# Inverses emitted in slices of four steps, keys' transposes as a stream of their own

## The chip, the cores and the metric

One core of a Trainium2 chip runs the kernel. The metric is the device time of one execution in microseconds (us), the median of three timed runs. One more execution was recorded by the hardware profiler; its trace is what is read here. "us" without a further word is time on the chip. The kernel also has a clock of its own, which exists only while the program is written out; its microseconds are called planned us.

## What is computed

One inference step of a hybrid decoder layer, for a prompt of 1024 tokens and 8 sequences of 4 new tokens, with model width 1024. The part around the change is the RWKV-7 branch with 16 heads of 64:

```python
def step(S, inp):                       # one token, all heads
    r_t, w_t, k_t, a_t, b_t, v_t = inp
    sa = jnp.einsum('bhij,bhj->bhi', S, a_t)
    S = S * w_t[:, :, None, :] + sa[..., :, None] * b_t[..., None, :] + v_t[..., :, None] * k_t[..., None, :]
    y = jnp.einsum('bhij,bhj->bhi', S, r_t)
    return S, y

z = rmsnorm(x) @ w_in                   # convolution, r/k/v/lora and gate columns
ya = conformer_conv(z) @ w_conv_out
yb = gated(group_norm(wkv7_scan(...))) @ w_rw_out
x = x + (sigmoid(g1) * ya + sigmoid(g2) * yb) @ w_mix_out
x = x + conv_ffn(rmsnorm(x))            # 1024 -> 6144 -> 3072 -> 1024
```

## The kernel before

The token recurrence is done in chunks of 64 tokens. In a chunk the recurrence is a triangular system, and its 64x64 matrix is inverted: two 32x32 diagonal blocks are inverted by forward substitution on VectorE, and the off-diagonal block is made from them on TensorE. The stage that does this, `mixer_b`, goes through 16 units (n = 0 to 15); a unit is four heads by 256 tokens, so it has 16 chunk matrices and 32 diagonal blocks of 32x32.

What a unit goes through, with the lines of the profile:

- `prep` (lines 880 to 985): five loads, decays and scaled keys E and BK on VectorE, ScalarE and GpSimd. It holds two waits, 6.0 and 8.0 planned us. Unit n may only start when chain n-3 is done.
- `stage` (from line 992): 16 matmuls of BK and E with 128 columns ("the keys"), evicted and masked into LQ (lines 1005 to 1013). Then the 32 diagonal blocks go to memory (dL, line 1019), come back as one 512 KB load that spreads each block over the partitions four times over (L, line 1021), and the substitution runs in 31 steps of two VectorE instructions, a product tm (line 1028) and a sum into X (line 1030), each step needing the step before. X goes to SBUF through ScalarE (Xs, line 1032), to memory (dX, line 1034) and back into LQ (line 1038). Last, BK is turned by 8 transposes in two halves, each after 0.5 planned us, and v by 4 more after a wait for chain n-2.
- `combine` (from line 1061): VectorE transposes of LQ (D11, line 1068), then two rounds of 16 matmuls with 32 columns.
- `chain` (from line 1090): the four chunks of a unit, one after another, each with four rounds of small matmuls and VectorE evictions between them (R, UV), because the state passes from chunk to chunk and from unit to unit.
- `group_norm`, the samples' own work, the layer norm of the convolution branch.

Each of these is a Python generator, a stream. `drive` writes the program: it asks the first stream in its list whose due time has come to emit its next piece, and when none is due it emits three matmuls of a filler, the weight projections of r, k, v and of the gates (`project_g`). The clock is advanced by each matmul's columns over 2.4 GHz, four times that for plain float32 operands. `yield 500` means: not before 0.5 planned us from now. A stream that waits for another's mark looks every 0.4 planned us (`wait`). Fillers remain to be emitted after the last chain.

The order in which code is emitted isn't the order on an engine. The tile framework hands the program to a scheduler that fills each engine's queue; where two instructions could go, the one emitted first goes first. On the chip each queue is then fixed and runs in order. All loads and stores are issued from SyncE (SP). The buffers that matter: one L, one tm, one Xs, one X in PSUM; three each of E, BK and LQ; two UV; two PSUM banks "w" that nearly every small product shares.

The streams and their list:

```python
self.drive([self.s_chain(), self.s_comb(), self.s_stage(), self.s_norm(), self.s_prep(), self.s_samples(), self.s_ln(), self.s_y(), self.s_shift()],
           self.fillers())
```

Of the kernel before, what the change touches and what calls it, by code (L numbers as in the profile page):

```python
# [31 lines left out]
class Net:  # L32
# [638 lines left out]
    def mixer_b(self):  # L671
        nc, a = self.nc, self.a
        self.wkv_consts()
        self.t2_left = self.T2N
        self.want = 0
        self.t_stage = {}
        self.st, self.pr, self.ch = {}, {}, {}
        with ExitStack() as e:
            self.t4 = self.pool(e, "t4b", 2)
            self.t2 = self.pool(e, "t2", self.T2N)  # L680
            self.e_sg = ExitStack()
            self.sg = self.pool(self.e_sg, "stage", 3, side="right")
            self.ln = self.pool(e, "lanes", 1)
            self.sm = self.pool(e, "small", 2)
            sp = self.pool(e, "samples")
            self.sG, self.sQK = (sp.tile([128, 4, 64], F32, name=x) for x in ("sG", "sQK"))
            self.sbv = sp.tile([128, 4, 32], F32, name="sbv")
            self.sUV = sp.tile([128, 8, 64], F32, name="sUV")
            self.sPC = sp.tile([128, 8, 8], F32, name="sPC")
            dram = lambda nm, m, w: [self.dr.tile([m, w], F32, name=f"{nm}{i}") for i in range(ND)]  # L690
            self.d_BT, self.d_S = dram("d_BT", 64, 128), dram("d_S", 128, 512)
            self.d_bv = [self.dr.tile([128, 2, TP], F32, name=f"d_bv{i}") for i in range(ND // 2)]
            self.drive([self.s_chain(), self.s_comb(), self.s_stage(), self.s_norm(), self.s_prep(), self.s_samples(), self.s_ln(), self.s_y(), self.s_shift()],
                       self.fillers())
            self.e_sg.close()

# [49 lines left out]
    def s_stage(self):  # L746
        for n in range(self.NH):
# [3 lines left out]
            self.done.add(("stage", n))  # L751
            self.t_stage[n] = self.clock

    def s_comb(self):
        for n in range(self.NH):
            yield from self.wait(("stage", n))
            yield max(0, self.t_stage[n] + self.TINV - self.clock)
            yield from self.combine(n)
            self.done.add(("comb", n))
# [227 lines left out]
    W_NIN, W_BV, W_GN, W_STAGE = 6000, 8000, 12000, 0  # L987
    W_LN = 14000
    SQ = (1, 1, 2, 1)
    TINV = 29750  # L990

    def stage(self, n):

        nc = self.nc
        E, BK, PC, nin, v = self.pr[n]
        LQ = self.sg.tile([128, 8, 128], F32, tag="LQ", name="LQ")
        for g in range(2):
            c4 = slice(4 * g, 4 * g + 4)
            for x in range(2):
                p, q = slice(64 * x, 64 * x + 64), slice(64 - 64 * x, 128 - 64 * x)  # L1000
                ps = self.pw_tile()
                pv = ps.rearrange("p (c t) -> p c t", t=128)
                for c in range(4):
                    self.mm(pv[:, c], BK[p, 4 * g + c], E[x][p, 4 * g + c], True, True)
                nc.vector.tensor_tensor(out=LQ[p, c4, 0:64], in0=pv[p, :, 0:64],
                                        in1=nin[p, c4].rearrange("p (c o) -> p c o", o=1).to_broadcast([64, 4, 64]), op=ALU.mult)
                nc.scalar.activation(out=LQ[p, c4, 64:128], in_=pv[p, :, 64:128], func=AF.Copy)  # L1007
                nc.scalar.activation(out=E[x][q, c4], in_=pv[q], func=AF.Copy)
                for w in (LQ[p, c4], E[x][q, c4]):
                    w = w.rearrange("p c (q t) -> p c q t", q=2)  # L1010
                    nc.gpsimd.affine_select(out=w, in_=w, pattern=[[0, 4], [1, 2], [1, 64]], compare_op=ALU.is_ge, fill=0.0,  # L1011
                                            base=-1, channel_multiplier=-1)
                yield 500

        dL = self.dr.tile([2, 2, 8, 32, 32], F32, name=f"dL{n}")
        dX = self.dr.tile([8, 4, 32, 32], F32, name=f"dX{n}")
        for x in range(2):
            for d in range(2):
                nc.sync.dma_start(out=dL[x, d].rearrange("c i j -> i c j"), in_=LQ[64 * x + 32 * d:64 * x + 32 * d + 32, :, 32 * d:32 * d + 32])
        L = self.ln.tile([128, 32, 32], F32, tag="L", name="L")  # L1020
        nc.sync.dma_start(out=L, in_=dL.rearrange("(o h) d c i j -> o (h d c) (i j)", o=1).to_broadcast([4, 32, 1024]))

        X = self.pw.tile([128, 512], F32, tag="x", name="x", bufs=1)[:, 0:256].rearrange("p (a t) -> p a t", t=32)
        tm = self.ln.tile([128, 8, 32], F32, tag="tm", name="tm")
        nc.vector.tensor_copy(out=X, in_=self.x0)
        for s in range(31):
            a, m = s // 4 + 1, 31 - s
            nc.vector.tensor_tensor(out=tm[:, :a, :m], in0=L[:, s:s + 1, s + 1:32].to_broadcast([128, a, m]),  # L1028
                                    in1=X[:, :a, s:s + 1].to_broadcast([128, a, m]), op=ALU.mult)
            nc.vector.tensor_tensor(out=X[:, :a, s + 1:32], in0=X[:, :a, s + 1:32], in1=tm[:, :a, :m], op=ALU.add)  # L1030
        Xs = self.ln.tile([128, 8, 32], F32, tag="X", name="X")
        nc.scalar.activation(out=Xs, in_=X, func=AF.Copy)
        for q in range(4):
            nc.sync.dma_start(out=dX[:, q].rearrange("a l t -> l a t"), in_=Xs[32 * q:32 * q + 32])
        for x in range(2):
            for d in range(2):
                p = 64 * x + 32 * d
                nc.sync.dma_start(out=LQ[p:p + 32, :, 32 * d:32 * d + 32],
                                  in_=dX.rearrange("a q l t -> (a q) l t")[:, 16 * x + 8 * d:16 * x + 8 * d + 8])

        for g in range(2):
            yield 500
            ps = self.pw_tile()
            for c in range(4):
                self.tr(ps[:, c * 128:(c + 1) * 128], BK[:, 4 * g + c], self.ident)
            nc.scalar.activation(out=BK[:, 4 * g:4 * g + 4], in_=ps.rearrange("p (c t) -> p c t", t=128), func=AF.Copy)
        yield from self.wait(*([("chain", n - 2)] if n > 1 else []))
        UV = self.sg.tile([128, 8, 2, 64], F32, tag="UV", name="UV", bufs=2)
        ps = self.pw_tile()
        for m in range(4):  # L1050
            self.tr(ps[:, m * 128:(m + 1) * 128], v[:, m // 2, m % 2 * 128:m % 2 * 128 + 128], self.ident)
        pv = ps.rearrange("p (m x t) -> p m x t", m=4, x=2)
        uv = UV.rearrange("p (m o) x t -> p m o x t", o=2)
        for o in range(2):
            for x in range(2):
                q = slice(64 - 64 * x, 128 - 64 * x)
                nc.scalar.activation(out=uv[q, :, o, x], in_=pv[64 * o:64 * o + 64, :, x], func=AF.Copy)
        self.st[n] = (E, LQ, BK, UV)
        self.t2_left += 1
# [622 lines left out]
```

## Time and profile before

| | |
|---|---|
| median of three runs | 2564.65 us |
| lowest, highest | 2553.85, 2574.9 us |
| the profiled execution's own time | 2538.03 us |
| its span in the trace | 2536.3 us |
| mean granted TensorE clock over the span | 0.926 |
| TensorE busy | 2367.6 us |
| VectorE busy | 1427.9 us |

The span is the time from the first to the last recorded instruction; 1.7 us of the execution lie around it. A granted clock of 1.00 is 2.4 GHz, 0.50 is 1.2 GHz, and a value between is a stretch that had both. PE is TensorE's matmuls, PEld its weight loads, DVE VectorE, ACT ScalarE, POOL GpSimd, SP the engine that issues the transfers. An entry such as "[5.07 <-DMA L<-dL]" says that the engine stood idle for 5.07 us before that instruction and what released it.

### The profile page before, as it was taken

What the parts mean: (1) busy time and instruction counts of PE and PEld (TensorE: products, weight loads), DVE (VectorE), ACT (ScalarE), POOL (GpSimd) and SP (SyncE); (2) the same over time, 40 slices, a digit from 0 to 9 for tenths busy, and PEclk for the clock granted to TensorE, in tenths of its full rate; (3) what the DMA queues carried; (4) which work ended last, traced back from release to release, by engine and by line L of the source; (5) the groups of instructions that cost most, each with busy time, mean ns of one, the idle gap of its engine ahead of it and who ended that gap; (6) DMA issues with size and microseconds to landing.
All of it is one profiled execution on the core that took longest, in us unless ns stands there. A gap on an engine that the chain in (4) does not pass through costs nothing.

```text
span 2536.3 us, 41660 instructions
## 1 busy us (share of the span) xinstructions
PE 2367.6 (93%) x16094; PEld 2140.9 (84%) x16094; DVE 1427.9 (56%) x3588; ACT 918.7 (36%) x1748; POOL 909.1 (36%) x879
## 2 busy tenths in 40 slices
PE   5889989999788799999989999999999999999998
PEld 4878888777676677777777899999999999999998
DVE  5799955586646674555464434465444534445345
ACT  4133433354244354454434322333222222223125
POOL 3332253244324443443333243433323323323333
PEclk9899987898688698999779999999999999999999
DMA  3223443243233333533323854431111111111111
GB/s 104 56 60 130 171 149 89 81 121 93 78 89 79 93 107 83 140 98 94 94 64 96 273 178 131 128 128 44 44 47 48 44 51 44 47 48 41 54 46 75
DMA packets 307640, 230.64 MB, mean 91 GB/s; under 512 B 90492, under 2 KB 287123, under 8 KB 306921
## 3 DMA queue, kind: packets, MB, share of 16 engines
q1 hardware_dynamic: 307185, 227.80, 31.1%
q8 instruction: 127, 2.08, 0.4%
q14 instruction: 72, 0.59, 0.1%
q0 software_dynamic: 256, 0.17, 0.0%
HBM read 157.45 MB, written 70.45 MB: 90 GB/s over the span
## 4 chain that ended last, share of the span: by engine, by line
PE 66%; DVE 7%; DMA 7%; POOL 3%; issue 2%; ACT 1%; SPq 1%; POOLq 0%; DVEq 0%; ACTq 0%
PE mm L54 52%; PE w L54 7%; DMA L<-dL 4%; PE c L54 2%; PE y L54 2%; PE w L61 2%; DVE tm L1028 1%; DVE x L1030 1%; DVE t L961 1%; DMA ga<-d_ga 0%; POOL BK L982 0%; POOL wlo L49 0%; POOL LQ L1011 0%; DVE lnQ L666 0%; DVE v L486 0%
## 5 line engine op out<-in xcount | busy, mean ns | idle before, releaser
L54 PE MATMUL mm<-hH,whi 128*128 128x352 f32 (+1 forms) x2568 | 887.6, 346 | 27.0 <-DVE bcol L496 11.2
L54 PE MATMUL mm<-hL,whi 128*128 128x352 f32 (+1 forms) x2568 | 866.2, 337 | 0.2 <-DVE hL L248 0.2
L54 PE MATMUL mm<-hH,wlo 128*128 128x352 f32 (+1 forms) x2568 | 862.7, 336 | 0.0
L54 PEld LDWEIGHTS mm<-hH,whi 128*128 128x128 f32 (+1 forms) x2568 | 499.4, 194 | 55.9 <-issue 14.1
L54 PEld LDWEIGHTS mm<-hL,whi 128*128 128x128 f32 (+1 forms) x2568 | 500.9, 195 | 11.2 <-DVE hL L248 0.5
L54 PEld LDWEIGHTS mm<-hH,wlo 128*128 128x128 f32 (+1 forms) x2568 | 500.6, 195 | 8.7 <-issue 0.2
L49 POOL TENSOR_TENSOR wlo<-wraw,whi 128x1024 fp32r<-128x1024 f32 (+2 forms) x123 | 292.5, 2378 | 462.0 <-ACT whi L48 427.9
L48 ACT ACTIVATE whi<-wraw 128x1024 fp32r<-128x1024 f32 (+2 forms) x123 | 126.0, 1025 | 366.8 <-PE mm L54 270.1
L1544 DVE SCALAR_TENSOR_TENSOR c<-u,par,c 128x1024 f32<-128x1024 f32 x96 | 167.0, 1739 | 55.6 <-ACT c L1540 55.6
L359 DVE SCALAR_TENSOR_TENSOR sg<-cu,par,sg 128x1024 f32<-128x1024 f32 x120 | 185.1, 1550 | 3.4 <-ACT sg L357 1.7
L1514 DVE TENSOR_TENSOR u<-mm,rs 128x352 f32<-128x352 f32 x144 | 73.2, 509 | 186.5 <-PE mm L54 186.3
L54 PE MATMUL mm<-fH,whi 128*128 128x352 f32 x504 | 163.4, 324 | 0.0
L1569 DVE TENSOR_TENSOR acc<-mm,acc 128x352 f32<-128x352 f32 x168 | 86.8, 523 | 135.0 <-PE mm L54 135.0
L54 PE MATMUL mm<-fH,wlo 128*128 128x352 f32 x504 | 162.7, 323 | 0.0
L54 PE MATMUL mm<-fL,whi 128*128 128x352 f32 x504 | 162.7, 323 | 0.0
L1028 DVE TENSOR_TENSOR tm<-L,x 128x60 f32<-128x60 f32 (+24 forms) x496 | 99.4, 200 | 79.7 <-DMA L<-dL 72.5
L1030 DVE TENSOR_TENSOR x<-x,tm 128x60 f32<-128x60 f32 (+24 forms) x496 | 105.0, 212 | 7.0
L1525 POOL COPY lr<-u 128x2 f32<-128x2 f32 x48 | 9.0, 187 | 276.3 <-DVE u L1514 267.6
L54 PE MATMUL w<-E,BK 64*128 64x128 f32 x512 | 90.7, 337 | 8.8 <-DVE tm L1028 3.4
L1011 POOL TENSOR_SCALAR_AFFINE_SELECT LQ<-LQ 64x512 f32<-64x512 f32 x64 | 44.1, 690 | 148.3 <-ACT LQ L1007 146.8
L54 PEld LDWEIGHTS mm<-fH,whi 128*128 128x128 f32 x504 | 94.8, 188 | 0.5
L54 PEld LDWEIGHTS mm<-fH,wlo 128*128 128x128 f32 x504 | 95.0, 188 | 0.0
(379 smaller groups left out, 3971.2 us busy)
## 6 DMA issues: line engine op xcount, KB each, us to landing
wraw<-w_in SPq DMA_DIRECT2D x50, 512.0 KB
wraw<-w_up SPq DMA_DIRECT2D x48, 512.0 KB
wraw<-w_down SPq DMA_DIRECT2D x32, 384.0 KB
L<-dL SPq DMA_DIRECT2D x16, 512.0 KB
d_alr<-la SPq DMA_DIRECT2D x8, 528.0 KB
d_cum<-lc SPq DMA_DIRECT2D x8, 528.0 KB
d_gout<-lg SPq DMA_DIRECT2D x8, 528.0 KB
d_k<-k SPq DMA_DIRECT2D x8, 528.0 KB
```

The costliest lines, as they stand in the source:

```text
L48: nc.scalar.activation(out=hi[:, :nk, :m], in_=raw[:, :nk, :m], func=AF.Copy)
L49: (lo_eng or nc.gpsimd).tensor_tensor(out=lo[:, :nk, :m], in0=raw[:, :nk, :m], in1=hi[:, :nk, :m].bitcast(F32), op=ALU.subtract)
L54: self.nc.tensor.matmul(out, l, r, start=start, stop=stop)
L61: self.nc.tensor.transpose(out, x, ident)
L359: nc.vector.scalar_tensor_tensor(out=c[:, 0:TP], in0=u[:, t:t + TP], scalar=self.col("conv_w", t * 4 + i), in1=c[:, 0:TP], op0=ALU.mult, o ...
L961: nc.vector.scalar_tensor_tensor(out=t1[:, u], in0=r[:, u], scalar=self.col("r_k", 2 * J + u), in1=km[:, u], op0=ALU.mult, op1=ALU.mult)
L1011: nc.gpsimd.affine_select(out=w, in_=w, pattern=[[0, 4], [1, 2], [1, 64]], compare_op=ALU.is_ge, fill=0.0, base=-1, channel_multiplier=-1)
L1028: nc.vector.tensor_tensor(out=tm[:, :a, :m], in0=L[:, s:s + 1, s + 1:32].to_broadcast([128, a, m]), in1=X[:, :a, s:s + 1].to_broadcast([12 ...
L1030: nc.vector.tensor_tensor(out=X[:, :a, s + 1:32], in0=X[:, :a, s + 1:32], in1=tm[:, :a, :m], op=ALU.add)
L1514: nc.vector.tensor_tensor(out=u[:, 2 + t0:2 + t0 + m], in0=p, in1=rs[:, t0:t0 + m], op=ALU.mult)
L1544: nc.vector.scalar_tensor_tensor(out=c[:, 0:TP], in0=u[:, t:t + TP], scalar=wt, in1=c[:, 0:TP], op0=ALU.mult, op1=ALU.add)
L1569: nc.vector.tensor_tensor(out=acc[i][:, s], in0=ps[:, :BW], in1=acc[i][:, s], op=ALU.add)
```

## The change

Three things are done. The 31 substitution steps, which were emitted in one piece right behind the load of L, are now emitted in eight slices: the first 6.0 planned us after the load (W_L), and each further slice of four steps 1.7 planned us after the one before (W_INV). The transposes of BK and v leave `stage` and become `turned`, driven by a stream `s_turned` of its own that starts as soon as the keys are masked. The combine's delay TINV behind the end of `stage` goes from 29.75 to 12.0 planned us, and it now waits for both marks. No instruction is added or taken away, and no tile or buffer changes.

```diff
-            self.drive([self.s_chain(), self.s_comb(), self.s_stage(), self.s_norm(), ...
+            self.drive([self.s_chain(), self.s_comb(), self.s_stage(), self.s_turned(), self.s_norm(), ...
...
+    def s_turned(self):
+        for n in range(self.NH):
+            yield from self.wait(("keys", n))
+            yield from self.turned(n)
+            self.done.add(("turned", n))
+
     def s_comb(self):
         for n in range(self.NH):
-            yield from self.wait(("stage", n))
+            yield from self.wait(("stage", n), ("turned", n))
             yield max(0, self.t_stage[n] + self.TINV - self.clock)
             yield from self.combine(n)
             self.done.add(("comb", n))
...
-    TINV = 29750
+    W_L = 6000
+    TINV = 12000
+    W_INV = 1700
...
                 yield 500
+        self.lq[n] = LQ
+        self.done.add(("keys", n))
 
         dL = self.dr.tile([2, 2, 8, 32, 32], F32, name=f"dL{n}")
...
         tm = self.ln.tile([128, 8, 32], F32, tag="tm", name="tm")
+        yield self.W_L
         nc.vector.tensor_copy(out=X, in_=self.x0)
         for s in range(31):
+            if s and s % 4 == 0:
+                yield self.W_INV
             a, m = s // 4 + 1, 31 - s
...
+    def turned(self, n):
+
+        nc = self.nc
+        E, BK, PC, nin, v = self.pr[n]
+        LQ = self.lq[n]
 
         for g in range(2):
             yield 500
```

What follows in `turned` is what stood at the end of `stage`: the transposes of BK, the wait for chain n-2, the transposes of v, the copies into UV, and the release of v's buffer.

## Rows read from the trace of the kernel before

**Rows 1.** The page's line of the granted TensorE clock in 40 equal slices of the span, 63.4 us each, in tenths (9 is 90% or more).

```profile
PEclk9899987898688698999779999999999999999999
```

**Rows 2.** Busy time over the stretch in which the 16 units run, counted from the start of the span. Columns: stretch, its length, then busy us of PE, PEld, DVE, ACT, POOL with counts, the mean granted clock, the transfers' share and GB/s.

```profile
360.00:1410.00 1050.00, 946.97 (x7510) 776.70 (x7509) 621.18 (x2359) 463.38 (x1054) 412.14 (x432) 0.85 0.37 96
```

**Rows 3.** What TensorE's matmuls waited for between 360 and 1410 us. Columns: us in total, times, longest.

```profile
PE w L54 <- DVE tm L1028: 18.9, 6, 6.0
...
PE w L61 <- DVE x L1030: 7.6, 1, 7.6
PE w L54 <- DVE x L1030: 7.5, 2, 7.2
PE c L54 <- DVE R L1126: 7.0, 7, 4.9
```

**Rows 4.** VectorE's groups of instructions by line between 360 and 1410 us, the two of the substitution: busy us and mean ns of one, then idle time just before them and what ended it.

```profile
L1030 DVE TENSOR_TENSOR x<-x,tm 128x60 f32<-128x60 f32 (+24 forms) x496 | 105.0, 212 | 7.0
L1028 DVE TENSOR_TENSOR tm<-L,x 128x60 f32<-128x60 f32 (+24 forms) x496 | 99.4, 200 | 79.7 <-DMA L<-dL 72.5
```

**Rows 5.** What VectorE waited for between 360 and 1410 us, the entry that concerns the load of L (us in total, times, longest).

```profile
DVE tm L1028 <- DMA L<-dL: 72.5, 13, 10.0
```

**Rows 6.** TensorE's instructions in order of time (start, duration, instruction, idle time before it and its releaser): nine of those before which it stood idle.

```profile
434.33 0.66 PE L54 MATMUL w<-D,LQ 32*32 32x32 f32 x16 [2.12 <-DVE tm L1028]
...
673.93 1.03 PE L54 MATMUL w<-D,LQ 32*32 32x32 f32 x16 [7.19 <-DVE x L1030]
...
740.85 0.66 PE L61 MATMUL w<-ident,sl 64*128 64x64 f32 x4 [7.58 <-DVE x L1030]
...
824.18 0.69 PE L54 MATMUL c<-R,LQ 64*64 64x64 f32 x8 [4.89 <-DVE R L1126]
...
877.00 0.66 PE L54 MATMUL w<-D,LQ 32*32 32x32 f32 x16 [1.90 <-DVE D L1068]
...
945.84 1.06 PE L54 MATMUL w<-D,LQ 32*32 32x32 f32 x16 [1.89 <-DVE D L1068]
...
1067.33 0.66 PE L54 MATMUL w<-D,LQ 32*32 32x32 f32 x16 [1.42 <-DVE D L1068]
...
1192.69 1.03 PE L54 MATMUL w<-D,LQ 32*32 32x32 f32 x16 [5.14 <-DVE tm L1028]
...
1331.87 1.03 PE L54 MATMUL w<-D,LQ 32*32 32x32 f32 x16 [6.04 <-DVE tm L1028]
```

**Rows 7.** Busy time by stretches of 4 us around the first of these idle times (columns as in rows 2).

```profile
430.00:434.00 4.00, 2.22 (x14) 1.93 (x13) 3.65 (x18) 0.10 (x1) 3.41 (x2) 1.00 0.28 49
434.00:438.00 4.00, 3.67 (x40) 3.27 (x41) 2.90 (x15) 1.15 (x2) 0.00 (x0) 0.65 0.65 191
438.00:442.00 4.00, 4.00 (x47) 3.37 (x46) 0.98 (x5) 1.01 (x3) 0.00 (x0) 0.50 0.29 83
...
458.00:462.00 4.00, 4.00 (x36) 2.87 (x35) 2.09 (x9) 0.77 (x2) 0.00 (x0) 0.86 0.00 0
```

**Rows 8.** VectorE's instructions in order of time where the substitution of unit 0 begins.

```profile
390.50 0.19 DVE L1028 TENSOR_TENSOR tm<-L,x 128x31 f32<-128x31 f32 x1 [5.07 <-DMA L<-dL]
390.60 0.58 DVE L486 SCALAR_TENSOR_TENSOR v<-mm,par,v 128x351 f32<-128x351 f32 x1
391.10 0.19 DVE L1030 TENSOR_TENSOR x<-x,tm 128x31 f32<-128x31 f32 x1
...
391.38 0.43 DVE L1005 TENSOR_TENSOR LQ<-w,nin 64x256 f32<-64x256 f32 x1
```

**Rows 9.** VectorE in order of time at the end of unit 7's substitution: the copy that prepares X for unit 8.

```profile
870.72 0.42 DVE L1025 COPY x<-x 128x256 f32<-128x256 f32 x1
```

**Rows 10.** Transfers in the order in which SP issued them (start and duration of the issue, not of the transfer): units 0 and 1, then units 7 and 8.

```profile
372.11 2.04 SPq L1019 DMA_DIRECT2D dL<-LQ  x4
...
394.39 4.62 SPq L1019 DMA_DIRECT2D dL<-LQ  x4
...
419.44 0.55 SPq L1021 DMA_DIRECT2D L<-dL  x1
420.09 2.65 SPq L1034 DMA_DIRECT2D dX<-X  x4
...
429.24 1.79 SPq L1038 DMA_DIRECT2D LQ<-dX  x4
...
870.69 1.78 SPq L1034 DMA_DIRECT2D dX<-X  x4
873.82 1.78 SPq L1038 DMA_DIRECT2D LQ<-dX  x4
...
884.76 0.57 SPq L1021 DMA_DIRECT2D L<-dL  x1
```

**Rows 11.** The chain of waits between 354 and 1410 us: the shortest and the longest of the loads of L in it (start, duration, from issue to landing).

```profile
419.44 8.86 DMA L<-dL
...
809.88 13.30 DMA L<-dL
```

**Rows 12.** All engines in order of time: the last keys of unit 0 on TensorE and the first VectorE transpose of its combine.

```profile
368.33 1.16 PE L54 MATMUL w<-E,BK 64*128 64x128 f32 x8
...
433.76 0.42 DVE L1068 STREAM_TRANSPOSE D<-LQ 32x256 f32<-32x256 f32 x1
```

**Rows 13.** What SP waited for before issuing, over the whole span: the store of X.

```profile
SPq L1034 <- ACT X L1032: 29.4, 11, 5.4
```

More of the change, by code (lines that the diff above doesn't have):

```diff
@@ L676, in mixer_b @@
         self.t_stage = {}
-        self.st, self.pr, self.ch = {}, {}, {}
+        self.st, self.pr, self.ch, self.lq = {}, {}, {}, {}
         with ExitStack() as e:
@@ L692, in mixer_b @@
             self.d_bv = [self.dr.tile([128, 2, TP], F32, name=f"d_bv{i}") for i in range(ND // 2)]
-            self.drive([self.s_chain(), self.s_comb(), self.s_stage(), self.s_norm(), self.s_prep(), self.s_samples(), self.s_ln(), self.s_y(), self.s_shift()],
+            self.drive([self.s_chain(), self.s_comb(), self.s_stage(), self.s_turned(), self.s_norm(), self.s_prep(), self.s_samples(), self.s_ln(), self.s_y(), self.s_shift()],
                        self.fillers())
```

## Prediction

> **What bounds the kernel now.** I read the granted clock over the whole span first. It is full at the end and dented in the slices that hold the 16 units [rows 1], so the time to be won or lost lies there; the change touches nothing else. Next the busy times of that stretch: in 1050 us TensorE has matmuls in flight for 947 us, so it is idle for 103 us, and its mean clock is 0.85 [rows 2]. A stretch at half clock does half the work, so the loss is (1 - 0.85) x 1050 = 157 us. VectorE with 621 us and ScalarE with 463 us [rows 2] have room. TensorE bounds the stage, and 260 of its 1050 us are lost to gaps and to the slow clock.
>
> The two losses belong together. Before 434.33 TensorE stands idle for 2.12 us [rows 6]. The clock is full in the 4 us with the gap, then 0.65, then 0.50 in five stretches, the first of which is shown, then 0.86 [rows 7]: 0.35 x 4 + 5 x 2 + 0.14 x 4 = 12 us lost behind 2 us of idle time. Over the whole stage each idle us brings 157 / 103 = 1.5 us more, so I price a gap at 2.5 times its length.
>
> Then I asked what ends the gaps. 18.9 + 7.6 + 7.5 = 34.0 us of the 103 end with a substitution step on VectorE [rows 3]. VectorE itself stands idle for 72.5 us in front of the first step, waiting for the load of L [rows 4], 13 times and up to 10.0 us [rows 5]. The load takes 8.9 to 13.3 us [rows 11]. A second family are the combines: seven of the nine gaps shown stand before their first matmuls, 2.12 + 7.19 + 1.90 + 1.89 + 1.42 + 5.14 + 6.04 = 25.7 us [rows 6]. The families overlap where both names stand in one row.
>
> **What the slices can move.** In the code the 62 instructions of a substitution stand in one block. On VectorE they don't: between the first product at 390.50 and its sum at 391.10 stands an eviction for a projection, and the keys of the next unit stand behind that [rows 8]. X for unit 8 was prepared at 870.72 [rows 9], 14 us before its load of L was even issued [rows 10]. So the scheduler puts a step where its inputs are expected, and emission only settles who goes first. The slices take from the inverse its precedence over what is emitted in the 6.0 + 7 x 1.7 = 17.9 planned us behind the load. Planned us are short: by the code unit 0's combine comes two times 0.5, then 29.75, then a look of up to 0.4 after its keys, 31 planned us, and it took 64 us, from 369.5 to 433.8 [rows 12], about 2 us each. The first slice is thus emitted some 12 us behind the keys and the last some 36 us. The substitution of unit 0 began 21 us behind them [rows 8, 12]. When L has landed, its first slice is older than the work then becoming ready, and still goes first.
>
> **The terms**, each against the profiled execution:
>
> - The wait for L. All 34.0 us gone with the clock behind them: 34.0 x 2.5 = 86 us less. Nothing changed, if the first step stays where L is expected: 0. I take 0 by the order just described [rows 8, 9]. The other end is for the range.
> - The 62 VectorE instructions of each unit stay, 99.4 + 105.0 us in all [rows 4]. They lie beside TensorE's fillers and add nothing.
> - The chain's evictions now precede later slices. TensorE waits 7.0 us for one of them, the copy R [rows 3]; a step is 0.2 us long [rows 4], so precedence removes tenths per meeting. Between 18 less (7.0 x 2.5) and 0; I take 0, by the length of a step.
> - The spacing of the keys. The stream `stage` is now occupied for 2.0 + 17.9 planned us per unit, so unit 1's keys can't follow unit 0's as closely as their stores do here, 372.1 to 394.4 [rows 10]. At 2 us per planned us they would come at about 372 + 40 = 412, and L behind them, so close to unit 0's dX at 420.09 that it may be issued behind it instead of 0.7 us ahead. Now that dX is followed by its reload after 9.2 us, against 3.1 us for unit 7, which has no L ahead of it [rows 10]. If so the gap before 434.33 and its slow clock go, 2 + 12 = 14 us. Between 14 less and 0; the spacing leaves it open, so I take half, 7 less. The delay of unit 1 itself costs nothing, since its L has to wait for the only L buffer until 419.44 anyway; without that cover it would be the 412 - 394 = 18 us by which the spacing grows, and TensorE has fillers for them.
> - The place of the combine. Before: 31 planned us behind the keys, later where chain n-2 is late. After: 17.9 + 12.0, plus a look, plus what each of eight waits overshoots until the next piece ends (three filler matmuls are 0.44 planned us, four key matmuls 0.85), together 32 to 37. It moves back by about 2 planned us, 4 us on the chip, which covers the gaps at 877.00, 945.84 and 1067.33, 1.90 + 1.89 + 1.42 = 5.2 us [rows 6], where emission sets the place. All seven gone would be 25.7 x 2.5 = 64 us less; none gone, 0; later inverses, more (the second rival). I take two of the three, 3.5 x 2.5 = 9 less.
> - `turned` issues the same 12 transposes and 6 copies, 0.4 planned us later at most. It holds back v and UV for chain n-2 as before. 0.
> - SP. The four stores of X and the four reloads are emitted 18 planned us later, so loads of weights and of the next unit come ahead of them. SP stood 29.4 us, 11 times, before that store, with those loads queued behind [rows 13]. TensorE's waits end on no load in this stage, so this is hidden by the fillers, 0; if a reload is pushed back, it is a combine's gap, which the second rival prices.
>
> Sum: -7 - 9 = -16 us. 2538 - 16 = 2522 us, a ratio of 0.994. The profiled execution is quicker than each of the three timed ones, so I apply the ratio to their median: 2564.65 x 0.994 = 2549 us. The three spread by 0.4% to either side, so a change within 1% is about what can't be told from none.
>
> **A rule against the gain.** Each load of L takes 8.9 to 13.3 us for its 512 KB [rows 11], and the small store behind one is held up [rows 10]. The Trainium skill, "DMA: Bandwidth & Descriptors", in "Why a DMA increments its semaphore by 16 and not by 1", says that the slowest dimension of a transfer's views sets how many of the 16 engines it uses. L's view begins with a dimension of 4, so at most four by that rule, wherever the load is emitted. The durations agree with it. By it the first term is the 0 that I take; had the wait depended on place, it would be up to 86 less.
>
> **The rivals.** *The inverse gives way* (faster): VectorE has older work ready whenever L is expected, the first step slips behind the load's landing, and half to all of 86 us goes; in the middle 64 us, 2564.65 x (2538 - 64) / 2538 = 2500 us. For it: VectorE is busy for 59% of the stage [rows 2], so it often has something to put first. Against it: the slice is still older than most of that. *The inverse ends too late* (slower): each step now yields to older work, and the reload of LQ comes later than the combine's place on TensorE. The place is the combine's first matmuls; the price is that of the gaps there, 25.7 / 7 x 2.5 = 9 us each; it decides once the last step slips by more than the 4 us that the combine moves back. Five of the other nine units so hit is 46 us, 2564.65 x 2584 / 2538 = 2611 us. For it: seven combines already wait. *It doesn't reorder anything*: VectorE's and TensorE's queues stay as they are but for single swaps, 2565 us. That lies within my 1%.
>
> **How the numbers follow.** Forecast with the last case, within 1% (2539 to 2590 us): 0.40. Inverse gives way: 0.36. Inverse too late: 0.24. There is this much on both sides because each gap costs 2.5 times itself and any swap on TensorE moves some. Range: from the first rival, short of its full 86 us (2478), to the second with six units instead of five: 2488 to 2618 us. Predicted is the likeliest case, 2549.
>
> **What would show it.** Right: VectorE still waits about 72 us for L, the first product still stands where L lands, three fewer combines with a gap, L of unit 1 issued behind dX of unit 0, idle time in the stage 95 to 103 us, and a clock near 0.86. Wrong on the faster side: the wait for L falls under 40 us and the stage's clock goes above 0.9. Wrong on the slower side: more than ten combines begin behind a gap.

## The result, and the profile after

The changed kernel takes 2588.64 us, the median of four runs (2574.71 to 2592.31); the kernel before, run beside it, 2559.25 us. The ratio over the fast runs, with executions in a second, slower state left out as in every ratio below, is 1.0127, with a 95% interval of 1.0083 to 1.0171 (the two medians alone divide to 1.0115). The change is slower by about 1.3%, inside the range of the prediction but on the other side of its 2549 us. The profiled execution took 2592.31 us, its span 2590.6 us, 54.3 us more than before.

The two traces differ by more than the two kernels. The traced execution of the kernel before, with 2538.03 us, is quicker than each of the 92 other executions of it that were timed beside the experiments below (2540.17 to 2583.56 us, median 2556.8); that of the changed kernel is the slowest of its four. About 30 of the 54 us are thus the change, the rest lies between executions of one and the same program. The clock shows it too: span x (1 - granted clock) is 188 us in the trace before and 238 us in the trace after, but 186 to 243 us over the 92 executions, median 211, and 219 to 246 us over the four of the changed kernel, median 234. By the medians 23 us of the slowdown are lost clock. What follows compares single traces, and the amounts are those of the traces.

First the granted clock over the span, in 40 slices, and then busy times by stretch: two stretches of the changed kernel, and the longer one of the kernel before (columns: stretch, length, busy us of PE, PEld, DVE, ACT, POOL with counts, granted clock, share and GB/s of the transfers).

```profile
PEclk9899987776867697999789799999999999999999
```

```profile
360.00:1410.00 1050.00, 947.88 (x7207) 777.76 (x7208) 597.66 (x2282) 446.09 (x1020) 402.25 (x427) 0.81 0.35 92
360.00:1560.00 1200.00, 1076.85 (x8068) 896.42 (x8069) 655.43 (x2412) 491.10 (x1097) 442.14 (x459) 0.82 0.38 104
```

```profile
360.00:1560.00 1200.00, 1091.62 (x8403) 920.03 (x8402) 680.04 (x2438) 501.82 (x1111) 468.16 (x473) 0.86 0.40 110
```

TensorE has as much in flight as before between 360 and 1410 us [rows 2], but at a clock of 0.81 instead of 0.85, and the row of units ends later (the last combine begins at 1429.61, shown below). So the longer stretch is compared: full-speed work is about 1091.62 x 0.86 = 939 us before and 1076.85 x 0.82 = 883 us after (950 and 888 us when it is summed over stretches of 4 us). The 56 to 61 us missing are about the 54 us of the span. TensorE is idle for 14.8 us more (1091.62 - 1076.85); the rest is the clock.

Now TensorE's idle time. Its waits in the changed kernel between 360 and 1410 us (us in total, times, longest):

```profile
PE w L54 <- DVE tm L1041: 23.5, 2, 12.5
PE w L54 <- DVE x L1043: 17.5, 4, 7.0
...
PE w L54 <- DVE D L1087: 7.1, 4, 3.4
```

and the same kernel's first matmuls of the combines, those that begin behind 1 us or more of idle time (start, duration, instruction, idle time and releaser; what lies between them is left out):

```profile
431.78 1.03 PE L54 MATMUL w<-D,LQ 32*32 32x32 f32 x16 [4.10 <-DVE x L1043]
556.01 0.69 PE L54 MATMUL w<-D,LQ 32*32 32x32 f32 x16 [3.38 <-DVE D L1087]
706.27 1.03 PE L54 MATMUL w<-D,LQ 32*32 32x32 f32 x16 [7.04 <-DVE x L1043]
850.84 1.03 PE L54 MATMUL w<-D,LQ 32*32 32x32 f32 x16 [3.85 <-DVE x L1043]
983.89 1.03 PE L54 MATMUL w<-D,LQ 32*32 32x32 f32 x16 [11.04 <-DVE tm L1041]
1250.03 1.03 PE L54 MATMUL w<-D,LQ 32*32 32x32 f32 x16 [12.47 <-DVE tm L1041]
1305.09 0.69 PE L54 MATMUL w<-D,LQ 32*32 32x32 f32 x16 [2.34 <-DVE D L1087]
1429.61 0.66 PE L54 MATMUL w<-D,LQ 32*32 32x32 f32 x16 [3.17 <-DVE D L1087]
```

Before there were seven, with 25.7 us [rows 6]; now eight, with 47.4 us, and two short ones of 0.58 and 0.79 us. The mean gap of the eight is 5.9 us instead of 3.7. The group's row, with the short ones in it, in the kernel before and in the changed one (busy us and mean ns, then idle time just before):

```profile
L54 PE MATMUL w<-D,LQ 32*32 32x32 f32 x512 | 25.6, 207 | 25.7 <-DVE tm L1028 13.3 <-DVE x L1030 7.2 <-DVE D L1068 5.2
```

```profile
L54 PE MATMUL w<-D,LQ 32*32 32x32 f32 x512 | 27.7, 214 | 48.8 <-DVE tm L1041 23.5 <-DVE x L1043 15.0 <-DVE D L1087 10.3
```

The longest gap in detail. VectorE ends the inverse of unit 12 at 1231.82 and prepares X for unit 13:

```profile
1231.82 0.17 DVE L1043 TENSOR_TENSOR x<-x,tm 128x8 f32<-128x8 f32 x1
1232.45 0.43 DVE L1036 COPY x<-x 128x256 f32<-128x256 f32 x1 [0.45 <-ACT X L1045]
1247.27 0.19 DVE L1041 TENSOR_TENSOR tm<-L,x 128x31 f32<-128x31 f32 x1 [14.40 <-DMA L<-dL]
...
1249.46 0.42 DVE L1087 STREAM_TRANSPOSE D<-LQ 32x256 f32<-32x256 f32 x1
```

SP issues, meanwhile (start and duration of the issue):

```profile
1232.88 2.08 SPq L1047 DMA_DIRECT2D dX<-X  x4
1235.06 0.57 SPq L1031 DMA_DIRECT2D L<-dL  x1
1235.73 0.42 SPq L47 DMA_DIRECT2D wraw<-w_in  x1
1236.33 9.45 SPq L1051 DMA_DIRECT2D LQ<-dX  x4
```

The load of L for unit 13 comes between the store and the reload of unit 12, and the four reloads need 9.45 us to be issued. On VectorE the combine of unit 12 stands behind the first steps of unit 13. TensorE has arrived at the combine at 1237.6 and stands still. What the clock does meanwhile is in the busy times by 4 us:

```profile
1240.00:1244.00 4.00, 0.00 (x0) 0.00 (x0) 0.00 (x0) 0.00 (x0) 0.00 (x0) 0.85 0.61 92
1244.00:1248.00 4.00, 0.00 (x0) 0.00 (x0) 0.62 (x4) 0.00 (x0) 0.00 (x0) 0.50 0.32 72
1248.00:1252.00 4.00, 1.98 (x18) 1.43 (x18) 3.27 (x15) 1.41 (x2) 2.10 (x1) 0.50 0.29 110
1252.00:1256.00 4.00, 4.00 (x25) 3.04 (x24) 1.52 (x5) 0.73 (x2) 1.28 (x2) 0.50 0.22 51
...
1276.00:1280.00 4.00, 4.00 (x30) 2.80 (x28) 2.32 (x11) 0.94 (x3) 0.27 (x1) 0.88 0.02 4
```

The clock falls inside the gap, and TensorE, busy again from 1250, works at half clock until 1276. I read all 300 stretches of 4 us between 360 and 1560 us in this way, for several kernels, and added up (1 - clock) x 4 us. Unbroken rows of slow stretches that hold the gap of a combine (1 us or more), or begin within 8 us behind one, are counted as "behind combines". The count says where the clock was slow, not why. The ratio is that of the timed runs, the other columns are from the one traced execution of each kernel:

| kernel | ratio | idle before combines | clock lost behind combines | clock lost elsewhere |
|---|---|---|---|---|
| before | 1 | 25.7 | 58 | 104 |
| after | 1.0127 | 48.8 | 125 | 93 |
| after, TINV 16000 | 1.0022 | 46.2 | 90 | 77 |
| after, TINV 20000 | 0.9915 | 14.4 | 48 | 106 |
| after, TINV 28000 | 0.9887 | 14.0 | 43 | 127 |
| before, TINV 37750 | 1.0079 | 25.0 | 43 | 179 |

Between the two traces the lost clock grows from 162 to 218 us, by 56 us, and by this count all of it lies behind the combines (+67; elsewhere -11). By the medians above about half of the 56 us lies between executions, not between the kernels.

### The profile page after: what moved, and what is told of

Its sections match the earlier page's. It is cut to its first block, busy times and chain, and to the rows that moved or that the text cites. A ratio compares the mean times of both kernels' runs of the same rounds, so it can differ in the third digit from the quotient of the medians.

```text
span 2590.6 us, 41636 instructions
## 1 busy us (share of the span) xinstructions
PE 2401.0 (93%) x16094; PEld 2166.8 (84%) x16094; DVE 1423.7 (55%) x3588; ACT 916.5 (35%) x1748; POOL 907.3 (35%) x879
## 4 chain that ended last, share of the span: by engine, by line
PE 49%; DMA 2%; DVE 2%; ACT 1%; POOL 1%; issue 0%; SPq 0%; POOLq 0%; DVEq 0%; ACTq 0%
PE mm L54 44%; PE w L54 2%; PE c L54 1%; DMA L<-dL 1%; PE y L54 1%; PE w L61 1%; POOL BK L988 0%; PE w L1527 0%; PE w L1442 0%; DMA cs<-d_cs 0%; DMA ga<-d_ga 0%; DVE t L967 0%; PE mm L1663 0%; PE w L1548 0%; DMA d_ma<-ga 0%
## 5 line engine op out<-in xcount | busy, mean ns | idle before, releaser
L54 PE MATMUL mm<-hH,whi 128*128 128x352 f32 (+1 forms) x2568 | 886.6, 345 | 20.2 <-DVE bcol L496 14.4
L1041 DVE TENSOR_TENSOR tm<-L,x 128x60 f32<-128x60 f32 (+24 forms) x496 | 99.6, 201 | 74.0 <-DMA L<-dL 66.1
L54 PE MATMUL w<-E,BK 64*128 64x128 f32 x512 | 97.2, 342 | 3.5 <-ACT E L1016 2.8
```

Source lines behind the costliest of these rows:

```text
L54: self.nc.tensor.matmul(out, l, r, start=start, stop=stop)
```

## The experiments

Three theories stood against each other at first, and a fourth from the second group of runs on. Theory 1: the next unit's first product waits for L on VectorE ahead of the combine's transposes. Theory 2: the slices give way, and the inverse ends later. Theory 3: any new emission deals the gaps anew, and the kernel before is a lucky deal. Theory 4: the combine is emitted too early against its inverse, so TensorE comes to it and waits. The inverse's length below is from the first product to the last sum on VectorE, in the mean of the 16 units.

**The two parts, each alone.** The transposes as a stream, with the substitution in one piece (against the changed kernel):

```diff
-    TINV = 12000
+    TINV = 30750
...
-        yield self.W_L
...
-            if s and s % 4 == 0:
-                yield self.W_INV
```

> The changed kernel without slices: the keys' transposes are a stream of their own, the substitution is emitted in one block right behind the load of L, and TINV is 30.75 planned us behind it, so that the combine is emitted where it was. Theory 1 (the next unit's first product, waiting for L, stands ahead of a combine's transposes on VectorE, and the new emission makes that wait longer): depends on the order dealt; gaps before combines 15 to 35 us. Theory 2 (slices give way and the inverse ends later): as the kernel before, within 0.5%, inverse of 38 to 39 us from first product to last sum. Theory 3 (any new emission deals the gaps anew): off by up to 1.5% to either side.

Measured 1.014 [1.008, 1.0199]; idle before combines 35.5 us. And the kernel before with the slices, the transposes still at the end of `stage`:

```diff
-    TINV = 29750
+    W_L = 6000
+    TINV = 11000
+    W_INV = 1700
...
+        yield self.W_L
...
+            if s and s % 4 == 0:
+                yield self.W_INV
```

> The kernel before with the slices (6.0 and 1.7 planned us) and TINV 11.0, the transposes still behind the substitution in the stage. Theory 2: slower by about the change's 1.3%, inverse of about 41 us. Theory 1: slower only if the waits for L in front of combines get longer than before. Theory 3: anything between 0.985 and 1.015.

Measured 1.0101 [1.0054, 1.0149]; idle before combines 46.0 us. Each part alone costs about what both cost together. The inverse takes 38.6 us before, 40.9 us in the changed kernel, 43.7 us with the slices alone and 35.7 us with the transposes alone. So theory 2 can't be the whole: without slices the inverse is shorter than before, and the slowdown is there. Nor do the two runs lose the same thing: by the count of the table the slices alone lose 101 us of clock behind combines and 109 us elsewhere, the transposes alone 56 and 160 us.

**The wait for L taken away.** In both kernels the load is cut into four, one for each copy of the blocks:

```diff
-        nc.sync.dma_start(out=L, in_=dL.rearrange("(o h) d c i j -> o (h d c) (i j)", o=1).to_broadcast([4, 32, 1024]))
+        for o in range(4):
+            nc.sync.dma_start(out=L[32 * o:32 * o + 32].rearrange("p i j -> p (i j)"), in_=dL.rearrange("h d c i j -> (h d c) (i j)"))
```

> The kernel before with the load of L cut into four loads of 32 partitions each, same bytes. By the estimate that such a load is spread over more transfer engines it lands in 4 to 6 us instead of 9 to 13. Theory 1: VectorE's wait for L falls from 72 to under 30 us, the idle time before combines from 26 to under 15, the time by 20 to 60 us. Theory 2: 0 to 20 us less. Theory 3: no direction.

> The changed kernel with the same cut. Theory 1: the wait for L falls from 66 to under 30 us, idle time before combines from 49 to under 20, and the kernel comes to within 10 us of the kernel before with that cut. Theory 2: it stays about 29 us behind it. Theory 3: no direction.

Measured 1.001 [0.9979, 1.004] for the kernel before with the cut and 1.0118 [1.0064, 1.0172] for the changed one. VectorE's waits between 360 and 1500 us, in that order:

```profile
DVE D L1069 <- DMA LQ<-dX: 37.3, 17, 6.1
DVE tm L1029 <- DMA L<-dL: 3.2, 3, 1.2
```

```profile
DVE D L1088 <- DMA LQ<-dX: 39.7, 18, 8.4
DVE tm L1042 <- DMA L<-dL: 3.3, 3, 1.2
```

The wait for L is gone (72.5 us before [rows 5]), and neither kernel is faster. What is late next is the reload: VectorE waits 37.3 and 39.7 us for it, and TensorE 30.4 and 42.9 us for the combines. In the form that the wait for L makes the changed kernel the slower one, theory 1 falls: the wait is gone in both, and they still lie 1.1% apart.

The run doesn't show what a sooner L would be worth, because the inverse doesn't begin sooner. In unit 1 of the kernel before with the cut (the first and the last of the four loads on SP, and the first product on VectorE):

```profile
428.48 0.49 SPq L1022 DMA_DIRECT2D L<-dL  x1
...
436.26 0.45 SPq L1022 DMA_DIRECT2D L<-dL  x1
```

```profile
447.82 0.19 DVE L1029 TENSOR_TENSOR tm<-L,x 128x31 f32<-128x31 f32 x1
```

The scheduler spread the four loads over SP's queue and put the first product later into VectorE's: it stands 14.9 us behind the first issue of L in the mean of the units, against 10.9 us with the single load (13.1 against 10.8 us in the changed kernel).

**How much a new order is worth by itself.** Two small shifts of the delay in the kernel before (`TINV = 31750`, `TINV = 27750`), and one of an unrelated stream (`W_LN = 14500` instead of 14000):

> The kernel before with TINV 31.75 instead of 29.75 planned us: each combine is emitted 2 planned us later, nothing else. With the load of L cut in four VectorE's wait for L fell to 3 us in both kernels and the difference between them stayed, so the wait for L isn't the cause. Theory 2 (slices give way): no slices here, within 0.4%. Theory 3 (any new emission deals the gaps anew, and the kernel before is a lucky deal): 0.5 to 1.5% slower with no structural reason. Theory 4 (later combines cost): slower by some 0.3% only.

> The kernel before with TINV 27.75: each combine 2 planned us earlier. Theory 3: 0.5 to 1.5% slower, as with 31.75. Theory 4, earlier combines cost because TensorE reaches them before their inverse is back: more idle time before combines than 26 us, and slower; with 31.75 less and faster.

> The kernel before with a delay of another stream, the convolution's layer norm, 14.5 instead of 14.0 planned us (W_LN). It has nothing to do with the inverses. Theory 3: off by 0.5 to 1.5%, more probably slower. Theories 2 and 4: within 0.4%.

Measured 1.0047 [1.0011, 1.0083], 1.0103 [1.003, 1.0177] and 1.0039 [1.0002, 1.0075]; idle before combines 31.2, 46.5 and 28.4 us. The two shifts that don't bring the combine forward cost 0.4 to 0.5%: that much of the 1.3% may be the loss of a lucky order (theory 3). Bringing it forward by 2 planned us costs 1.0%, with as much idle time before the combines as in the changed kernel. But moving it back by the same amount didn't gain, as theory 4 would have it: in the kernel before, either way costs.

**Closer slices, the combine in its place.** The changed kernel with `W_INV = 1500` and `TINV = 13400`:

> The changed kernel with 1.5 instead of 1.7 planned us between slices and TINV 13.4, so that the combine stays where it is. Theory 3: anything between 0.3 and 2% slower than the kernel before. Theory 2: 1.0 to 1.4% slower, like the changed kernel.

Measured 1.0213 [1.0147, 1.0279], idle before combines 44.1 us. The slices are emitted closer together and the kernel is slower still. On the chip the inverse is not shorter but longer, 43.8 us against 40.9, so the run says nothing against theory 2. With the combine in its planned place the kernel is about 0.9% slower than the changed one (the two intervals overlap); so much may hang on a small shift of the emission here.

**The combine later.** The changed kernel with `TINV` alone raised, from 12000 to 16000, 20000 and 28000:

> The changed kernel with TINV 16000, half of the way from 12000 to 20000. Theory 4: between the two, ratio 0.997 to 1.008, idle time in front of the combines 25 to 40 us. Theory 3 (the 0.992 of 20000 was luck): anywhere from 1.000 to 1.013, with no order in the three.

> The changed kernel with one constant changed: TINV 20000 instead of 12000, so every combine is emitted 8 planned us later than in the changed kernel, with the inverses in the same slices. Theory 4 (the changed kernel emits its combines too early for their inverses, so TensorE comes to them and waits): TensorE's idle time in front of the combines' first matmuls falls from 48.8 us to under 30, the clock between 360 and 1560 us rises to 0.85, ratio to the kernel before 0.995 to 1.006. Theory 3 (any new emission deals the gaps anew, and the kernel before holds a lucky deal): 1.000 to 1.008 and an idle time that may lie anywhere between 25 and 45 us. A third view, that the combine's place is worth nothing and the slices cost by themselves: 1.010 to 1.015 as in the changed kernel.

> The changed kernel with TINV 28000, a further 8 planned us later than 20000. Theory 4: the combines no longer wait for an inverse at all (idle time under 10 us in front of them), but the chains come later too and each unit's successor with them; ratio 0.985 to 1.000, with the gain no larger than that of 20000 if the chain of units becomes the bound. Theory 3: 1.000 to 1.010.

Measured 1.0022 [0.9981, 1.0063], 0.9915 [0.9876, 0.9955] and 0.9887 [0.9813, 0.996]. The combines' first matmuls with 20000, then with 28000:

```profile
L54 PE MATMUL w<-D,LQ 32*32 32x32 f32 x512 | 23.5, 199 | 14.4 <-DVE x L1043 11.0 <-DVE D L1087 3.3
```

```profile
L54 PE MATMUL w<-D,LQ 32*32 32x32 f32 x512 | 22.6, 201 | 14.0 <-DVE tm L1041 6.3 <-DVE D L1087 5.4 <-DVE ry L666 1.9
```

The time falls in order over four places, and so does the clock lost behind combines (125, 90, 48, 43 us, table above; with gaps under 1 us counted too, the last two change places, 48 and 55). The idle time itself does not fall in step: with 16000 it is still 46.2 us. The two latest places beat the kernel before, and with 20000 the inverse takes 42.0 us, longer than in the changed kernel, which speaks against theory 2. To see whether 0.9915 is luck, the same place with a fresh order (`W_LN = 14500` besides):

> The changed kernel with TINV 20000 and, besides, a wait of an unrelated stream (W_LN, the layer norm of the convolution branch) of 14500 instead of 14000 planned us, which deals the order of the whole stage anew without touching the combine's place. Theory 4: the gain stays, idle time in front of the combines under 22 us, ratio 0.988 to 1.000. Theory 3 (0.992 was a lucky deal): back to 1.003 to 1.013.

Measured 0.998 [0.9942, 1.0019], idle before combines 30.9 us. Of the 2.1% between 12000 and 20000, 1.5% stay. The slowdown doesn't come back, but the size of the gain depends on the order.

**The old anchor.** Before, TINV ran from the end of the transposes, which wait for chain n-2. The changed kernel, with the combine also not sooner than 29.75 planned us behind them:

```diff
...
             self.done.add(("turned", n))
+            self.t_turn[n] = self.clock
...
-            yield max(0, self.t_stage[n] + self.TINV - self.clock)
+            yield max(0, self.t_stage[n] + self.TINV - self.clock, self.t_turn[n] + 29750 - self.clock)
```

> The changed kernel, in which the combine also may not be emitted sooner than 29.75 planned us after the end of the unit's transposes: the place that it had in the kernel before, where those transposes, with their wait for the chain of unit n-2, stood in front of that delay. The slices and the stream of transposes stay. Theory 4, in the form that the change lost the delay behind chain n-2: the idle time in front of the combines falls to about 25 to 32 us, ratio 0.997 to 1.006. Theory 3: 1.000 to 1.010 with no relation to the place. Slices cost by themselves: 1.010 to 1.015.

Measured 1.0139 [1.0097, 1.0181], idle before combines 48.7 us. Theory 4 in this form had 0.997 to 1.006. The lost delay behind chain n-2 is not the cause by itself; what helped in the runs above was a later place in every unit.

**The combine freed from its inverse.** The reload goes to a scratch tensor, in both kernels, so the combine works on the blocks that were not inverted and depends on the keys alone; the work and the transfers stay:

```diff
+        Q = self.dr.tile([128, 8, 32], F32, name=f"Q{n}")
...
-                nc.sync.dma_start(out=LQ[p:p + 32, :, 32 * d:32 * d + 32],
+                nc.sync.dma_start(out=Q[p:p + 32],
```

> The kernel before with one part of the computation changed: the inverted blocks are computed, stored and loaded back as before, but into a scratch tensor in memory instead of into LQ, so the combine works on the blocks that were not inverted and depends on the keys alone. The amount of work and of transfers is the same. Theory 4: no combine waits for its inverse any more, the idle time in front of the combines' first matmuls falls from 25.7 us to under 8, and at 2.5 us for each idle us some 45 us are gained, ratio 0.98 to 0.985. Theory 3: the idle times reappear elsewhere, ratio 0.995 to 1.005.

> The changed kernel with the same part left out: the inverted blocks return to a scratch tensor and the combine depends on the keys alone. Theory 4: the idle time in front of the combines falls from 48.8 us to under 8, the cost of the change goes with it, and this kernel and the kernel before with the same part left out agree within 0.5%, both at 0.98 to 0.985 of the kernel before. Theory 2 (the slices themselves cost, on VectorE): the changed kernel stays 1% above the other one. Theory 3: both near 1.000, with no relation to each other.

Measured 1.0019 [0.9989, 1.0049] and 0.994 [0.9902, 0.9979]. Without the dependence the changed kernel's slowdown is gone (1.0127 to 0.994), as theory 4 has it. But theory 4 had both kernels at 0.98 to 0.985, and the kernel before gains nothing, although the idle time before its combines falls to 1.3 us. TensorE's waits in it, between 360 and 1500 us, show where they went:

```profile
PE y L54 <- DVE UV L1146: 18.7, 7, 5.1
PE y L54 <- DVE UV L1135: 16.4, 7, 4.0
```

These are the evictions in the chain (3.0 and 5.7 us in the kernel before), and the clock between 360 and 1560 us is 0.83 instead of 0.86. In that trace the clock loses 209 us between 360 and 1560 us, none of it behind combines by the count of the table, where the kernel before lost 162 in all. A gap that is taken away can come back in the chain.

**The later place without the other parts.** The kernel before with `TINV = 37750`; the transposes alone with `TINV = 38750`; the slices alone with `TINV = 19000`. All put the combine about 39 planned us behind the keys, as 20000 does in the changed kernel:

> The kernel before with one constant changed: TINV 37750 instead of 29750, so every combine is emitted 8 planned us later, the same shift that took the changed kernel from 1.013 to 0.992, but without slices and with the transposes in the stage. Theory 4 in its plain form (only the combine's place counts): idle time in front of the combines under 15 us, ratio 0.985 to 0.995. If slices and separate transposes are what lets the later combine pay: ratio 1.000 to 1.010, as with the two smaller shifts of this constant. Theory 3: between 1.000 and 1.010 too, but with no fall of the idle time in front of the combines.

> The changed kernel without the slices (the 31 steps in one piece right behind the load of L, the transposes still a stream of their own), and with TINV 38750 behind the end of the stage, 39 planned us behind the keys. That is the place that the combine has in the changed kernel with TINV 20000 (38 to 40), which measured 0.992, and in the kernel before with TINV 37750, which measured 1.008. If the separate transposes are what makes the late place pay (in the kernel before the delay starts behind the wait for chain n-2, so a longer one slows the row of units): 0.988 to 0.998, idle time in front of the combines under 16 us. If the slices are: 1.003 to 1.012. If it is only a fresh deal each time: anywhere from 1.000 to 1.010.

> The kernel before with the slices alone (the transposes stay at the end of the stage, behind the wait for chain n-2) and with TINV 19000 instead of the 11000 of the run with the slices alone, which measured 1.010: the combine again about 39 planned us behind the keys. If the slices are what makes the late place pay: 0.988 to 0.998, idle time in front of the combines under 16 us, clock between 360 and 1560 us 0.86 to 0.87. If the separate transposes are: 1.003 to 1.012, clock 0.82 to 0.83. A fresh deal each time: anywhere from 1.000 to 1.010.

Measured 1.0079 [1.0041, 1.0117], 1.0139 [1.0091, 1.0187] and 1.0055 [1.0007, 1.0102]; idle before combines 25.0, 31.9 and 35.0 us. None gains. In the kernel before with the later place the clock lost behind combines does fall, from 58 to 43 us, but elsewhere it grows from 104 to 179 us. So in these runs the later place pays only where slices and separate transposes are together. Why it needs both isn't settled.

## Why the prediction was wrong

**What bounds the kernel: right.** The time is made in the stretch of the units, by idle time and slow clock. The price of a gap doesn't hold. By the table 58 us of clock were lost behind 25.7 us of gaps before, 2.3 us for each and not 1.5; the changed kernel has 2.6 (125 / 48.8), and with TINV at 16000 and 20000 it is 1.9 and 3.3. And when 24.4 us of these gaps were taken away from the kernel before, nothing was gained: an average over one trace isn't what one gap less is worth.

**The wait for L, 0: right.** It stayed, 66.1 us against 72.5 [rows 5]:

```profile
DVE tm L1041 <- DMA L<-dL: 66.1, 13, 14.4
```

The run with the cut shows more. There the rival "the inverse gives way" has its condition, a first product behind other work and a wait for L under 40 us, and nothing is gained. The end at -86 us, and with it that rival's 0.36, took a releaser's name for the cause. In unit 12 the last of the four reloads was issued by 1245.8, and L landed at 1247.27: the reload was due at almost the same time.

**The spacing of the keys, -7: wrong in sign.** L of unit 1 still goes ahead of unit 0's dX:

```profile
415.43 0.56 SPq L1031 DMA_DIRECT2D L<-dL  x1
416.08 1.99 SPq L1047 DMA_DIRECT2D dX<-X  x4
...
426.20 2.00 SPq L1051 DMA_DIRECT2D LQ<-dX  x3
```

The order on SP is the one of before [rows 10]; the gap of that combine is 4.10 us against 2.12 [rows 6], with 29 us of clock lost behind it against 12 [rows 7]. So by that count this combine costs 2 + 17 = 19 us more, where 7 less were forecast.

**The place of the combine, -9: the step that failed.** I counted planned us behind the keys in each unit and found 32 to 37 against 31, so 4 us of cover more. Measured as TensorE's work at full speed (busy time x clock, in the 4 us stretches) from the first store of dL to the combine's first matmul, it is 61.2 us before and 57.5 after, in the mean of the 16 units: 3.7 us sooner. From the inverse's last step to the combine, the cover proper, it is 12.3 us before and 9.9 after (12.3 again with TINV 20000). Idle time before combines grew by 23.1 us, where two or three gaps should have gone. The planned distance of two streams didn't tell the order of queues that a scheduler fills by its own expectations. The smaller cover is not the whole account: with TINV at 16000 the cover is 12.4 us again, and the idle time is still 46.2 us.

**`turned`, 0, and SP, 0.** The separate transposes alone gave 1.014, which stands against the 0 for `turned`. That the combine's old delay began behind the wait for chain n-2 is in the prediction ("later where chain n-2 is late"), but without a number. The run with that delay restored shows that this alone doesn't explain the slowdown. For SP the text said that a reload pushed back is a combine's gap; unit 12 shows one.

**The rivals.** "The inverse ends too late" had the right place and side, and 2611 us against 2589 measured. The side was partly luck. It was to decide once the last step slips by more than 4 us, and the inverse is 2.3 us longer. Its trigger was wrong too: not five more combines, but one more (three with the short gaps), with longer gaps and, between the two traces, 56 us more of lost clock. Its test, more than ten combines behind a gap, would have missed it. The upper end of the range, six such units, works out to 2620 us and not 2618. "It doesn't reorder anything" underrated that a swap of no meaning costs 0.4 to 0.5% here, and 0.7% from 0.9915 to 0.998. A part of the 1.3% may be no more than that.

**What stays open.** The combine's place is shown to move the changed kernel: from 1.013 to between 1.002 and 0.989 in four runs with a later one. Why the change as a whole was slower stays open in part. It isn't shown that the place is the only cause: the idle time with 16000 was as large as with 12000, and the same place gave nothing where only one part of the change was there.

## What to carry to other kernels

A delay that was tuned against an emission order belongs to that order: when work is sliced or moved to a stream of its own, scan the delay again before judging the change; here the same slices went from 1.3% slower to 1.1% faster by one constant. Before pricing a wait by its releaser, ask what was due right behind it: cutting the wait for L from 72.5 to 3.2 us was worth nothing. A price for a gap that is an average over one trace has to be tried on a run that takes the gap away. And before single traces are compared, place each among the other executions of its kernel, and have at hand the cost of a change that means nothing.

## What the runs showed of the hardware

A single load of 512 KB with a fourfold leading dimension took 8.86 to 13.30 us from issue to landing [rows 11]. In the kernel before with the cut VectorE waited for L in three units; there the last of the four loads of 128 KB, to 32 partitions each, released it 2.5 to 3.5 us after its issue began (issued at 953.51, first product at 955.97 in one of them). The rule that the prediction cites from the Trainium skill ("DMA: Bandwidth & Descriptors", in "Why a DMA increments its semaphore by 16 and not by 1") would let such a load use all 16 engines, since its views begin with a dimension of 32. But a quarter of the bytes could give the shorter time as well; no row shows the number of engines, so no run here decides it.

The granted clock of TensorE fell inside a gap of 12.47 us, and it stayed at 1.2 GHz for 26 us of work behind it, 17 us lost in all. Behind a gap of 2.12 us in the kernel before 12 us of clock were lost [rows 7], and behind one of 4.10 us in the changed kernel 29 us: the loss doesn't go in step with the gap.
